# Head halves alternating in the matmuls of a recurrence: preparation and scan output of an RWKV-7 mixer, with a zero-padded operand

## The chip, the cores and the metric

The kernel runs on one core of one Trainium2 chip. The metric is the device time of one execution in microseconds (us). The kernel before takes 4488.92 us, the median of 3 runs from 4473.94 to 4512.09.

## What is computed

Two layers of a backbone with four head groups side by side (neighbourhood attention, latent attention, RWKV-7 time mixing in both directions, differential attention), each followed by a gated MLP, over 1024 latent and 256 context tokens of width 1024 in float32. The change lies in the RWKV-7 group, whose reference is a scan over tokens, per head a 64 x 64 state S:

```python
def rwkv7_scan(r, decay, k, v, a, b, s0, reverse):
    def step(S, inp):
        r_t, w_t, k_t, v_t, a_t, b_t = inp
        sa = jnp.einsum('bhij,bhj->bhi', S, a_t)
        S = S * w_t[:, :, None, :] + sa[..., None] * b_t[:, :, None, :] + v_t[..., None] * k_t[:, :, None, :]
        return S, jnp.einsum('bhij,bhj->bhi', S, r_t)
    ...
```

with decay, a and k made per token from a small low-rank projection (`w0[d] + jnp.tanh(wd) @ w_up[d]`, `a0[d] + ad @ a_up[d]`). It runs forwards and backwards (d = 0, 1), over the context first, then over the latent tokens; layer 1 needs no output for the context.

## The kernel before, in words

The scan is done in chunks of 64 tokens. Four heads are held as two pairs p; a pair's two heads are the halves e = 0, 1 of the 128 partitions (partitions 64e to 64e + 63). A slot is 128 tokens, two chunks; ten slots per layer. The index u = 2p + c names pair and chunk.

`mix` builds one layer's work from generators that are pulled in turn at given rates: a main one (projections, then attention) and sides. A scheduler then sets the order in which each engine issues its instructions, by its own estimate of their times and by what they wait for; every engine works its queue in order. The sides that the change touches:

- `prep_gen`, preparation, beside the projections (lines L140 to L142, tiles psd and psv). Per slot, `load` (L312) fetches the slot's columns into z and the inputs of the low-rank projection into zm, 33 partitions (32 and a row of ones, memset in L319); `partA` (L322) makes, for j = 0 (decay) and j = 1 (a), four matmuls into a PSUM tile pu each (L330), both with partitions 0 to 32 as operands. `partB` then makes BK and ARM; `gram(d)` (L432) multiplies them per half e, four matmuls of 64 partitions into a tile pg each (L437), first all of e = 0, then all of e = 1; `gout` masks the results into NT, RB and ARM; `tb(d)` (L451) transposes BK per half into pbt (L456). PSUM tiles of preparation come from two pools of two buffers. A slot ends with stores to DRAM (rnt, rsg).
- `lanes_gen` inverts small triangular blocks with VectorE (L543, L544) and merges them with 32 x 32 matmuls (L576, L578).
- `rw_step_gen`, the scan, 20 steps per layer, beside the attention (L788 logits psL, L958 exp, L996 transposes psT, L1017 products psV) and the modulation matmuls of later stages (L1541, adaps). A step: eight matmuls into pd (L653), ScalarE copies them to Dt (L656), eight into psa (L665), ScalarE and VectorE copy the halves into V1 (L667, L668), eight into pss (L674), VectorE makes the next state from pss and tmp (L682). V1 holds, for each e, psa's half on the partitions of e and a copy of VS's other half on the others (L649, on GpSimd, which also makes tmp, L659). Then comes the step's output py: for each direction d, pair p and half e one matmul over all 128 partitions (L692: VS by ARM, output on the 64 partitions of e) and one over the 64 partitions of e alone that adds to it (L693: V1 by RB). ScalarE copies py out (L697). In the step's PSUM tile pall, pss takes the place of pd, and py that of psa.

A matmul of float32 operands appears in the trace as two records of TensorE (two passes), a transpose as one.

```python
for e in range(2):
    r = slice(64 * e, 64 * e + 64)
    MM(py[r, d, p], VS[:, c, e, d, p], ARM[:, d, e, u, 64:P], start=True, stop=False)
    MM(py[r, d, p], V1[r, e, d, p], RB[r, d, u], start=False, stop=True)
```

Of the kernel before, what the change touches and what calls it, by code (L numbers as in the profile page):

```python
# [17 lines left out]
P = 128  # L18
# [22 lines left out]
class K:  # L41
# [241 lines left out]
    def prep_gen(self, l, rw, pool, psA, psB, F):  # L283
# [6 lines left out]
        uwa = pool.tile([33, 2, 512], F32, tag="rwuwa", name="rwuwa")  # L290
        nc.sync.dma_start(uwa, A["rwuwa"][l])
# [20 lines left out]
        def load(sl):  # L312
            s = self.SLOT[sl]
            z = pool.tile([P, 3, 2, P], F32, tag="sz", name="sz", bufs=2)
            zm = pool.tile([33, 2, P], F32, tag="szm", name="szm", bufs=2)
            nc.sync.dma_start(z, self.rzd[:, :, :, s * P:(s + 1) * P])
            for j in range(2):
                nc.sync.dma_start(zm[0:32, j], self.rzm[32 * j:32 * j + 32, s * P:(s + 1) * P])
            nc.gpsimd.memset(zm[32:33], 1.0)  # L319
            st[sl] = dict(z=z, zm=zm)  # L320

        def partA(sl):  # L322
# [4 lines left out]
            for j in range(2):  # L327
                pu = pst([P, 4, P], "pu")
                for dp in range(4):
                    MM(pu[:, dp], uwa[:, j, dp * P:(dp + 1) * P], zm[:, j], start=True, stop=True)  # L330
                ps.append(pu)
# [61 lines left out]
        def partB(sl):  # L393
# [38 lines left out]
            def gram(d):  # L432
                for e in range(2):
                    r = slice(64 * e, 64 * e + 64)
                    g[e] = psb([P, 4, P], "pg")
                    for u in range(4):
                        MM(g[e][:, u], BKf[r, d, u, 64 * e:64 * e + P], ARf[r, d, e, u], start=True, stop=True)  # L437
# [13 lines left out]
            def tb(d):  # L451
                for e in range(2):
                    r = slice(64 * e, 64 * e + 64)
                    g[2 + e] = psb([P, 4, 64], "pbt")
                    for u in range(4):
# [143 lines left out]
    def rw_step_gen(self, l, pool, sgp, yp, psp, ptag, need_ctx, F):  # L599
# [7 lines left out]

        def seg(i):
# [26 lines left out]
        for step in range(20):  # L635
# [32 lines left out]
            nc.vector.tensor_copy(V1[64:128, 1], psa[64:128])  # L668
            yield
# [14 lines left out]
            if i < 2 and not need_ctx:  # L684
                yield
                continue
            for d in range(2):
                for p in range(2):
                    u = 2 * p + c
                    for e in range(2):  # L690
                        r = slice(64 * e, 64 * e + 64)
                        MM(py[r, d, p], VS[:, c, e, d, p], ARM[:, d, e, u, 64:P], start=True, stop=False)  # L692
                        MM(py[r, d, p], V1[r, e, d, p], RB[r, d, u], start=False, stop=True)  # L693
# [1592 lines left out]
```

## Time and profile before

| | us |
|---|---|
| time, median of 3 runs (lowest, highest) | 4488.92 (4473.94, 4512.09) |
| profiled execution, span from first to last instruction | 4497.2 |
| TensorE busy | 4274.2 (95%) |
| VectorE busy | 2883.1 (64%) |
| ScalarE busy | 1984.4 (44%) |
| GpSimd busy | 754.3 (17%) |
| mean granted TensorE clock | 0.942 of full speed |

The profile is that of one execution on the chip. The profiled execution's own time is given by its span alone, which lies within the range of the timed runs. Matmuls overlap each other, and their ends are modelled, so a busy share of TensorE isn't a share of its peak; the distance between the starts of two matmuls is measured. Preparation runs from about 100 to 560 us (layer 0) and 2440 to 2860 us (layer 1), the scan from 600 to 1000 and from 3000 to 3325 us.

### The profile page before, as it was taken

How to read it: one execution, taken by the hardware profiler on the slowest of the kernel's cores; microseconds unless marked ns; L12 is line 12 of the kernel's file. 1: busy time of each engine (PE TensorE's matmuls, PEld its weight loads, DVE VectorE, ACT ScalarE, POOL GpSimd, SP SyncE). 2: the span in 40 equal slices, each digit the busy share in tenths (PEclk: the TensorE clock that was granted, in tenths of full speed). 3: DMA queues.
4: the chain of work that ended last, by engine and by line, in shares of the span. 5: the costliest groups of instructions: out<-in, count | busy, mean ns of one | idle time of the engine just before them, and what ended most of it. 6: DMA issues, size and time to landing. Idle time of an engine off the chain costs nothing.

```text
span 4497.2 us, 76564 instructions
## 1 busy us (share of the span) xinstructions
PE 4274.2 (95%) x29152; PEld 3473.1 (77%) x29152; DVE 2883.1 (64%) x5946; ACT 1984.4 (44%) x4386; POOL 754.3 (17%) x1224
## 2 busy tenths in 40 slices
PE   6999979999999999899998999979999999999998
PEld 4887857677677778788887887857786777788998
DVE  6678675546576766655556668675556676657666
ACT  4444434334465544433334444434434555434443
POOL 3244121112211011100001334121112101111000
PEclk7999978889999999999998999978899999999999
DMA  6344685553433243221213334685434432333322
GB/s 207 131 136 163 188 230 170 175 157 109 131 98 114 77 129 115 84 64 61 66 62 118 130 129 162 191 252 171 159 89 129 135 95 80 116 104 130 95 93 77
DMA packets 422598, 575.77 MB, mean 128 GB/s; under 512 B 109078, under 2 KB 287638, under 8 KB 420696
## 3 DMA queue, kind: packets, MB, share of 16 engines
q1 hardware_dynamic: 422232, 570.88, 41.1%
q8 instruction: 230, 3.77, 0.3%
q14 instruction: 136, 1.11, 0.1%
HBM read 430.84 MB, written 139.92 MB: 127 GB/s over the span
## 4 chain that ended last, share of the span: by engine, by line
PE 78%; DVE 11%; DMA 5%; issue 2%; ACT 2%; SPq 1%; POOL 1%; POOLq 0%; DVEq 0%; ACTq 0%
PE psm L140 12%; PE psm L141 12%; PE psm L142 11%; PE psV L1017 6%; PE psT L996 5%; PE psd L140 2%; PE psd L141 2%; PE psd L142 2%; PE psL L788 2%; DVE lpr L543 2%; PE pall L693 2%; PE pall L692 2%; PE pso L140 1%; PE pso L142 1%; PE pso L141 1%
## 5 line engine op out<-in xcount | busy, mean ns | idle before, releaser
L141 PE MATMUL psm<-h_l,whi 128*128 128x512 f32 (+1 forms) x2112 | 711.1, 337 | 9.1 <-DVE h_l L258 9.0
L140 PE MATMUL psm<-h_h,whi 128*128 128x512 f32 (+1 forms) x2112 | 713.7, 338 | 4.0 <-ACT h_h L257 4.0
L142 PE MATMUL psm<-h_h,wlo 128*128 128x512 f32 (+1 forms) x2112 | 709.2, 336 | 0.0
L1873 DVE SCALAR_TENSOR_TENSOR x<-psm,mod,x 128x258 f32<-128x258 f32 (+2 forms) x616 | 326.8, 555 | 285.2 <-PE psm L142 284.8
L958 ACT ACTIVATE sm_P<-psL,sm_n 128x512 f32<-128x512 f32 (+1 forms) x672 | 392.5, 593 | 251.7 <-DVE sm_n L949 225.2
L947 DVE TENSOR_REDUCE sm_m<-psL 128x1 f32<-128x512 f32 (+1 forms) x640 | 354.5, 579 | 180.8 <-PE psL L788 90.0
L141 PEld LDWEIGHTS psm<-h_l,whi 128*128 128x128 f32 x2112 | 399.4, 189 | 54.3 <-DVE h_l L258 12.1
L140 PEld LDWEIGHTS psm<-h_h,whi 128*128 128x128 f32 x2112 | 399.5, 189 | 53.9 <-ACT h_h L257 5.7
L142 PEld LDWEIGHTS psm<-h_h,wlo 128*128 128x128 f32 x2112 | 399.2, 189 | 43.8 <-issue 0.3
L140 PE MATMUL psm<-gh,dhi 128*128 128x510 f32 (+3 forms) x1056 | 364.3, 347 | 8.6 <-ACT mb L1837 4.0
L133 ACT ACTIVATE whi<-wst 128x1024 fp32r<-128x1024 f32 x176 | 186.5, 1060 | 403.3 <-PE psm L141 380.0
L141 PE MATMUL psm<-gl,dhi 128*128 128x510 f32 (+3 forms) x1056 | 357.2, 339 | 0.0
L142 PE MATMUL psm<-gh,dlo 128*128 128x510 f32 (+3 forms) x1056 | 356.9, 338 | 0.0
L134 DVE TENSOR_TENSOR wlo<-wst,whi 128x1024 fp32r<-128x1024 f32 x176 | 214.7, 1220 | 174.7 <-ACT whi L133 174.6
L996 PE MATMUL psT<-ident,sm_P 128*128 128x128 f32 x1744 | 303.9, 297 | 9.2 <-DVE sm_P L986 5.3
L1017 PE MATMUL psV<-PT,V 128*64 128x128 f32 x3488 | 308.0, 290 | 1.3 <-DVE sm_n L949 0.6
L1017 PEld LDWEIGHTS psV<-PT,V 128*64 128x64 f32 x3488 | 215.7, 141 | 85.6 <-issue 67.6
L996 PEld LDWEIGHTS psT<-ident,sm_P 128*128 128x128 f32 x1744 | 212.1, 150 | 76.2 <-issue 28.5
L140 PEld LDWEIGHTS psm<-gh,dhi 128*128 128x128 f32 x1056 | 199.4, 189 | 42.5 <-ACT a L1829 8.7
L1006 ACT ACTIVATE PT<-psT 128x512 f32<-128x512 f32 (+2 forms) x300 | 152.8, 526 | 153.7 <-PE psT L996 151.1
L142 PEld LDWEIGHTS psm<-gh,dlo 128*128 128x128 f32 x1056 | 200.1, 189 | 21.7
L141 PEld LDWEIGHTS psm<-gl,dhi 128*128 128x128 f32 x1056 | 200.2, 190 | 17.6 <-issue 0.5
(381 smaller groups left out, 9575.6 us busy)
## 6 DMA issues: line engine op xcount, KB each, us to landing
wst<-in_w_up_dram SPq DMA_DIRECT2D x176, 512.0 KB
wst<-in_w_down_dram SPq DMA_DIRECT2D x88, 512.0 KB
adw<-in_ada_w_dram SPq DMA_DIRECT2D x80, 512.0 KB
SG<-rsg SPq DMA_DIRECT2D x40, 896.0 KB
wst<-in_w_out_dram SPq DMA_DIRECT2D x96, 256.0 KB
rsg<-ARM SPq DMA_DIRECT2D x20, 1024.0 KB
K<-dfk SPq DMA_DIRECT2D x16, 960.0 KB
wst<-in_w_rw_dram SPq DMA_DIRECT2D x28, 512.0 KB
```

What stands on the lines that cost most here:

```text
L133: nc.scalar.activation(hi[:, :n], st[:, :n], AF.Copy)
L134: nc.vector.tensor_tensor(out=lo[:, :n], in0=st[:, :n], in1=hi[:, :n].bitcast(F32), op=ALU.subtract)
L140: mm(out, ah, bh, start=first, stop=False)
L141: mm(out, ah, bl, start=False, stop=False)
L142: mm(out, al, bh, start=False, stop=last)
L543: TT(out=pr[:n, 0:t, 0:t], in0=XT[:n, 0:t, 0:t], in1=M[:n, None, 0:t, t].to_broadcast([n, t, t]), op=ALU.mult)
L947: nc.vector.tensor_reduce(out=m[:, j, i:i + 1], in_=src, axis=AX.X, op=ALU.max)
L958: ACT(Pt[:, off:off + n], s["L"][j][t][:, to:to + n], AF.Exp, bias=neg, accum_out=sm[:, j, i:i + 1])
L996: nc.tensor.transpose(pt[:, j], Ph[:, (bb + j) * P:(bb + j + 1) * P], self.ident)
L1006: ACT(dst, src, AF.Copy)
L1017: nc.tensor.matmul(s["po"][64 * h:64 * h + 64, 0], V[:, kts[i], h], s["PT"][h][:, i], start=i == 0, stop=i == nk - 1, tile_position=(0, 64 ...
L1873: STT(out=x[:, s:e], in0=ps[:, s:e], scalar=mod[:, v, 40 + m:41 + m], in1=x[:, s:e], op0=ALU.mult, op1=ALU.add)
```

## The change

The two inputs of the low-rank projection lie on different partition halves now (zm and uwa: j = 0 on partitions 0 to 32, j = 1 on 64 to 96), and in pu, gram and tb the inner loop runs over the halves, so that consecutive matmuls in the source go to different row halves of the array. In the scan output, both matmuls with VS come first and then both that add to them, and the second operand V1 is replaced by SZ, a tile with V1's half on the partitions of e and zeros on the others, zeroed once per layer and filled by two GpSimd copies per step. The second matmul so reads all 128 partitions, as the first does.

```diff
-        uwa = pool.tile([33, 2, 512], F32, tag="rwuwa", name="rwuwa")
-        nc.sync.dma_start(uwa, A["rwuwa"][l])
+        uwa = pool.tile([P, 512], F32, tag="rwuwa", name="rwuwa")
+        for j in range(2):
+            nc.sync.dma_start(uwa[64 * j:64 * j + 33], A["rwuwa"][l][:, j])
...
-            zm = pool.tile([33, 2, P], F32, tag="szm", name="szm", bufs=2)
+            zm = pool.tile([P, P], F32, tag="szm", name="szm", bufs=2)
             nc.sync.dma_start(z, self.rzd[:, :, :, s * P:(s + 1) * P])
             for j in range(2):
-                nc.sync.dma_start(zm[0:32, j], self.rzm[32 * j:32 * j + 32, s * P:(s + 1) * P])
-            nc.gpsimd.memset(zm[32:33], 1.0)
+                nc.sync.dma_start(zm[64 * j:64 * j + 32], self.rzm[32 * j:32 * j + 32, s * P:(s + 1) * P])
+                nc.gpsimd.memset(zm[64 * j + 32:64 * j + 33], 1.0)
...
             for j in range(2):
-                pu = pst([P, 4, P], "pu")
-                for dp in range(4):
-                    MM(pu[:, dp], uwa[:, j, dp * P:(dp + 1) * P], zm[:, j], start=True, stop=True)
-                ps.append(pu)
+                ps.append(pst([P, 4, P], "pu"))
+            for dp in range(4):
+                for j in range(2):
+                    r = slice(64 * j, 64 * j + 33)
+                    MM(ps[j][:, dp], uwa[r, dp * P:(dp + 1) * P], zm[r], start=True, stop=True)
...
             def gram(d):
                 for e in range(2):
-                    r = slice(64 * e, 64 * e + 64)
                     g[e] = psb([P, 4, P], "pg")
-                    for u in range(4):
+                for u in range(4):
+                    for e in range(2):
+                        r = slice(64 * e, 64 * e + 64)
                         MM(g[e][:, u], BKf[r, d, u, 64 * e:64 * e + P], ARf[r, d, e, u], start=True, stop=True)
...
             def tb(d):
                 for e in range(2):
-                    r = slice(64 * e, 64 * e + 64)
                     g[2 + e] = psb([P, 4, 64], "pbt")
-                    for u in range(4):
+                for u in range(4):
+                    for e in range(2):
+                        r = slice(64 * e, 64 * e + 64)
                         nc.tensor.transpose(g[2 + e][:, u], BKf[r, d, u, 64 * e:64 * e + P], self.ident[r, r])
...
+        def step_y(i):
+            return i >= 2 or need_ctx
+
+        SZ = pool.tile([P, 2, 2, 2, 64], F32, name="SZ", bufs=1)
+        for e in range(2):
+            nc.gpsimd.memset(SZ[64 - 64 * e:128 - 64 * e, e], 0.0)
+
...
             nc.vector.tensor_copy(V1[64:128, 1], psa[64:128])
+            if step_y(i):
+                for e in range(2):
+                    nc.gpsimd.tensor_copy(SZ[64 * e:64 * e + 64, e], V1[64 * e:64 * e + 64, e])
...
-            if i < 2 and not need_ctx:
+            if not step_y(i):
...
                     u = 2 * p + c
+                    r = [slice(64 * e, 64 * e + 64) for e in range(2)]
                     for e in range(2):
-                        r = slice(64 * e, 64 * e + 64)
-                        MM(py[r, d, p], VS[:, c, e, d, p], ARM[:, d, e, u, 64:P], start=True, stop=False)
-                        MM(py[r, d, p], V1[r, e, d, p], RB[r, d, u], start=False, stop=True)
+                        MM(py[r[e], d, p], VS[:, c, e, d, p], ARM[:, d, e, u, 64:P], start=True, stop=False)
+                    for e in range(2):
+                        MM(py[r[e], d, p], SZ[:, e, d, p], RB[:, d, u], start=False, stop=True)
```

In the changed kernel the lines lie lower: pu is L333, gram L440, tb L460, the scan's pd L664, psa L676, the SZ copies L682, pss L688, the output L706 and L708.

The order of TensorE at the first scan output of layer 0, before. SG is the tile in which ARM, RB and BT are loaded, V_5908 the V1 of that step:

```order
L674 MATMUL pall<-V_5908,SG 64x64 x8
L788 MATMUL psL<-K,Q 128x512
L788 MATMUL psL<-K,Q 128x256
L692 MATMUL pall<-SG,VS 64x64
L693 MATMUL pall<-SG,V_5908 64x64
L692 MATMUL pall<-SG,VS 64x64
L693 MATMUL pall<-SG,V_5908 64x64
```

The same place in the changed kernel:

```order
L1011 MATMUL psT<-ident,sm_P 128x128 x4
L1556 MATMUL adaps<-adw,sc_60 32x256 x4
L1032 MATMUL psV<-PT,V 64x128 x8
L706 MATMUL pall<-SG,VS 64x64 x2
L708 MATMUL pall<-SG,SZ 64x64 x2
L706 MATMUL pall<-SG,VS 64x64 x2
L708 MATMUL pall<-SG,SZ 64x64 x2
```

The sixteen matmuls went one by one between the two lines; now two of L706 (e = 0, 1) and two of L708 follow each other.

The order of TensorE at the first gram of layer 0, before (pg_1140 is the tile of e = 0, pg_1145 of e = 1):

```order
L142 MATMUL psd_1313<-H0_h0_101,wlo_1123 128x512
L330 MATMUL pu_1172<-szm_1076,rwuwa_904 128x128 x4
L437 MATMUL pg_1140<-ARM_1082,BK_1081 128x128 x4
L437 MATMUL pg_1145<-ARM_1082,BK_1081 128x128 x4
L344 MATMUL pk_1218<-sel2_420,ksq_1196 128x2 x2
```

And now (pg_1143 is the tile of e = 0, pg_1144 of e = 1):

```order
L333 MATMUL pu_1171<-szm_1078,rwuwa_904 128x128 x4
L440 MATMUL pg_1143<-ARM_1085,BK_1084 128x128 x2
L440 MATMUL pg_1144<-ARM_1085,BK_1084 128x128 x2
L440 MATMUL pg_1143<-ARM_1085,BK_1084 128x128
L440 MATMUL pg_1144<-ARM_1085,BK_1084 128x128
L440 MATMUL pg_1143<-ARM_1085,BK_1084 128x128
L440 MATMUL pg_1144<-ARM_1085,BK_1084 128x128
L346 MATMUL pk_1221<-sel2_420,ksq_1199 128x2 x2
```

The halves alternate five times here, not seven times as in the source. At other places the scheduler puts the four of e = 0 ahead of the four of e = 1, as before.

The order of GpSimd in the scan of layer 0, before (o_ss is the sum of squares of the differential attention's output, V1 the L649 copies, stmp the products of L659):

```order
L649 COPY V1_6696<-VS_6338 64x256 x2
L1039 TENSOR_TENSOR o_ss_7016<-o_ss_7016,mhalf_68 128x2
L1040 TENSOR_TENSOR o_ss_7016<-o_ss_7016,rec_6374 128x2
L659 TENSOR_TENSOR stmp_6698<-VS_6338,W_6339 64x256 x2
L649 COPY V1_7116<-VS_6338 64x256 x2
L1037 TENSOR_TENSOR o_ss_7325<-o_ss_7325,rec_6658 128x2
```

And now:

```order
L670 TENSOR_TENSOR stmp_6545<-VS_6085,W_6086 64x256 x2
L1054 TENSOR_TENSOR o_ss_7355<-o_ss_7355,mhalf_68 128x2
L632 COPY W_7232<-Wc_94 128x2x2 x2
L1055 TENSOR_TENSOR o_ss_7355<-o_ss_7355,rec_6684 128x2
L682 COPY SZ_5885<-V1_6543 64x256 x2
L660 COPY V1_7144<-VS_6360 64x256 x2
L670 TENSOR_TENSOR stmp_6724<-VS_6360,W_6361 64x256 x2
L682 COPY SZ_5885<-V1_6722 64x256 x2
```

The two SZ copies of a step come in between the products of that step and the V1 copies for a later one, behind what o_ss work stands there.

## Rows read from the trace of the kernel before

**Rows 1.** The page's part 1: engine, busy us, share of the span, instructions.

```profile
PE 4274.2 (95%) x29152; PEld 3473.1 (77%) x29152; DVE 2883.1 (64%) x5946; ACT 1984.4 (44%) x4386; POOL 754.3 (17%) x1224
```

**Rows 2.** Busy time by stretch: length, engines, granted clock, DMA share, GB/s.

```profile
100.00:560.00 460.00, 442.50 (x2930) 370.10 (x2929) 326.56 (x588) 210.57 (x442) 147.33 (x212) 0.96 0.49 156
600.00:1000.00 400.00, 378.08 (x3598) 271.99 (x3599) 223.51 (x531) 155.58 (x463) 66.33 (x131) 0.82 0.61 181
1000.00:1400.00 400.00, 392.47 (x2514) 285.28 (x2512) 266.01 (x720) 206.07 (x541) 69.80 (x85) 0.97 0.38 112
3000.00:3325.00 325.00, 317.17 (x3183) 233.60 (x3183) 179.66 (x450) 140.46 (x415) 54.81 (x118) 0.88 0.54 162
```

**Rows 3.** Chain that ended last, shares by line: 600 to 1000, 3000 to 3325.

```profile
by line: PE psT L996 12.7%; PE psV L1017 12.2%; PE pall L693 11.8%; PE pall L692 11.7%; PE adaps L1541 7.5%; PE psL L788 5.7%; PE psL L140 4.6%; PE pall L653 3.5%; PE psL L141 3.4%; PE psL L142 3.4%; DVE sm_m L947 3.2%; DMA Q<-dfq 3.1%; PE 
...
by line: PE psT L996 14.8%; PE psV L1017 14.7%; PE pall L693 10.7%; PE pall L692 10.4%; PE psL L788 6.7%; PE adaps L1541 5.9%; PE psL L140 5.5%; PE psL L142 4.3%; PE psL L141 4.3%; PE pall L653 3.7%; PE pall L665 3.5%; PE pall L674 2.6%; DV
```

**Rows 4.** L674's durations (ns min/median/max); TensorE's timeline, its first row at half clock.

```profile
L674 PE MATMUL pall<-V,SG x640: 219/222/369, 618.5 to 3320.0; 128*64 128x64 f32 x160
...
618.51 1.12 PE L674 MATMUL pall<-V,SG 128*64 128x64 f32 x16 [1.35 <-DVE V L668]
...
945.76 1.31 PE L1017 MATMUL psV<-PT,V 128*64 128x128 f32 x18
...
953.55 0.69 PE L674 MATMUL pall<-V,SG 128*64 128x64 f32 x16
...
955.49 0.33 PE L692 MATMUL pall<-SG,VS 128*64 128x64 f32 x2
955.75 0.32 PE L693 MATMUL pall<-SG,V 64*64 64x64 f32 x2
...
960.04 1.97 PE L996 MATMUL psT<-ident,sm_P 128*128 128x128 f32 x8
```

**Rows 5.** Busy time in the 36 blocks of L692 and L693: first, last, sum.

```profile
622.57:629.02 6.45, 6.45 (x33) 4.58 (x32) 6.38 (x8) 0.00 (x0) 3.51 (x4) 0.50 1.09 242
...
3320.03:3324.09 4.06, 4.06 (x37) 2.98 (x33) 0.00 (x0) 0.00 (x0) 0.00 (x0) 1.00 0.00 0
sum 163.75, PE 163.27 PEld 118.90 DVE 61.32 ACT 30.65 POOL 34.06; mean PE 4.54 PEld 3.30 DVE 1.70 ACT 0.85 POOL 0.95
```

**Rows 6.** Timeline of VectorE and ScalarE: V1's second half, an exp.

```profile
950.73 0.43 DVE L668 COPY V<-pall 64x256 f32<-64x256 f32 x1 [0.98 <-ACT V L667]
...
956.39 0.68 ACT L958 ACTIVATE sm_P<-psL,sm_n 128x512 f32<-128x512 f32 x1
```

**Rows 7.** Busy time in the 22 stretches at half clock: first, last, sum.

```profile
672.10:682.40 10.30, 10.30 (x61) 7.91 (x59) 3.85 (x6) 3.28 (x12) 2.90 (x4) 0.50 0.72 178
...
3324.30:3327.70 3.40, 3.40 (x14) 2.95 (x12) 1.85 (x3) 0.28 (x1) 0.00 (x0) 0.50 0.35 104
sum 170.90, PE 168.50 PEld 121.50 DVE 62.35 ACT 53.20 POOL 22.64; mean PE 7.66 PEld 5.52 DVE 2.83 ACT 2.42 POOL 1.03
```

**Rows 8.** Timeline of TensorE in preparation, at full clock, with the next start.

```profile
115.03 2.02 PE L330 MATMUL pu<-szm,rwuwa 33*128 33x128 f32 x16
...
169.79 1.71 PE L437 MATMUL pg<-ARM,BK 64*128 64x128 f32 x16
171.43 0.50 PE L142 MATMUL psd<-H_h,wlo 128*128 128x512 f32 x1
...
233.96 1.16 PE L437 MATMUL pg<-ARM,BK 64*128 64x128 f32 x8
235.04 0.38 PE L140 MATMUL psv<-whi,H_h 128*128 128x256 f32 x1
```

**Rows 9.** Groups by line: out<-in, shapes, count, busy us, mean ns, idle before.

```profile
L437 PE MATMUL pg<-ARM,BK 64*128 64x128 f32 x640 | 85.8, 294 | 11.4 <-POOL ARM L405 11.4
L649 POOL COPY V<-VS 64x256 f32<-64x256 f32 x80 | 37.1, 467 | 181.6 <-PE pall L693 67.8 <-issue 54.4 <-DMA VS<-rvt 39.7
```

**Rows 10.** Waits of GpSimd: total us, times, longest.

```profile
POOL o_ss L1037 <- DVE o_ss L1035: 189.3, 30, 27.8
```

## The prediction

> **What bounds the kernel now.** I read the page's engine line first: TensorE is busy for 95% of the span, every other engine far less [rows 1]. That number is a modelled one, so the next view is the busy time by stretch [rows 2]. While the scan runs (600 to 1000 us in layer 0, 3000 to 3325 us in layer 1) TensorE is busy 378 of 400 and 317 of 325 us, VectorE at most 56%, ScalarE at most 43%, GpSimd 17%. The stretch behind it, 1000 to 1400, has the same attention without the scan, and TensorE is as full there, but its granted clock is 0.97 against 0.82 and 0.88 with the scan. Third, the chain that ended last in the two scan stretches [rows 3]: the scan output's two lines, L692 and L693, hold 23.5% of the 400 us (94 us) and 21.1% of the 325 (69 us). So these matmuls stand on the path nearly whole. Fourth, the timeline of one block tells why [rows 4]: each row is two records (one float32 matmul is two passes), L692 uses a 128x64 tile of the array and L693 a 64x64 tile, and the next row begins 0.26 us later; a whole block takes 4.06 us for its 32 records [rows 5], 127 ns each. L674, sixteen records of 128x64 whose output halves alternate, needs 0.69 us in all: without the last one's own 0.22 us (its median duration) that is 31 ns from start to start. Same operand sizes, a quarter of the time; the tile shape that changes at each pair is the difference.
>
> **The change part by part.**
>
> *Scan output.* Before, 16 matmuls per step go 128x64, 64x64, 128x64 and so on: 16 changes of shape. After, L708 reads all 128 partitions of SZ, whose other half is zero, so all 16 have one shape, and e alternates in pairs, which is the form of L674. There are 36 blocks (20 steps in layer 0, 16 in layer 1, where the two context segments need no output). The windows over them sum to 163.75 us, 4.55 each; one at full clock takes 4.06 [rows 5]. A new block at full clock: 32 records by 31 ns, about 1.0 us, and 0.2 for one change of shape at its entry (the 0.26 us of a pair less 2 x 31 ns): 1.2. With the present mix of clocks (4.55 / 4.06 = 1.12) 36 blocks take 48 us. Removed: 163.75 - 48 = 116 us of TensorE.
>
> How much of that stays a gain? After the block that starts at 955.49 come eight transposes of sm_P at 960.04 [rows 4]; an exp for such a tile begins at 956.39 and takes 0.68 [rows 6]. If the block ends at 956.7, they may stand 0.4 us for that exp and about as long for the next: some 0.7 of 3.35 us saved is lost again. So I keep four fifths: 93 us. The bounds are all of it (116, as VectorE and ScalarE are half idle) and half of it (58).
>
> *The clock.* Between 652 and 1000 us and between 3010 and 3330 us the granted clock fell to half (1.2 of 2.4 GHz) 22 times, in stretches of 170.9 us together [rows 7], and each of the 22 begins inside one of these blocks or at most 1.1 us behind it. The blocks' own excess over full clock is 163.75 - 36 x 4.06 = 17.6 us. L674's sixteen take 1.12 us instead of 0.69 at half clock [rows 4], so half clock costs 38% of the time spent in it; the 17.6 us thus are 46 us at half, of which 13 belong to two blocks in the slow beginning of the stage (the first takes 6.45 [rows 5]). So 170.9 - 33 = 138 us of other work ran at half clock, and 52 us come back if the falls end with the blocks. Other small matmuls stay in these stages (L653, L665, L674, the 32-column adaps), and a TensorE that now and then waits may lose its clock as well. I take two thirds: 35 us; bounds 0 and 52.
>
> *Gram, projection and transposes in preparation.* The source alternates e, but the scheduler decides the order of issue, and counted in the order of the changed program it keeps this only in part. Of the 40 gram calls (eight matmuls, 16 records), 22 had their halves apart before and 18 joined with one alternation; after, 10 are apart, 6 have one, 14 three, 8 five and 2 seven. For pu, matmuls followed by one of the other tile go from 14 to 98 of 160. For the transposes pbt from 0 to 5 of 320: that edit all but disappears. Prices: a gram half alone takes 1.08 us, two apart 2.16; joined with one alternation 1.64 [rows 8]. A full alternation doesn't occur before; its bounds are 1.0 (two streams wholly beside each other) and 1.64. I take 1.3 for three, 1.15 for five, 1.0 for seven: before 22 x 2.16 + 18 x 1.64 = 77, after 10 x 2.16 + 6 x 1.64 + 14 x 1.3 + 8 x 1.15 + 2 x 1.0 = 61, which saves 16 us of the 85.8 us that L437 is busy [rows 9]. pu is 16 records in 2.02 us and all on one half of the rows [rows 8]; halved where it alternates, 20 calls save about 12 us. In preparation TensorE is busy 442 of 460 us [rows 2], but VectorE 71% and each slot ends in a store and a load, so I count half: 14 of 28 us; bounds 0 and 28.
>
> *What is added.* Two copies V1 to SZ per step on GpSimd, 0.467 us each by the like copy L649 [rows 9]: 72 copies, 34 us on an engine that has 334 us free in the first scan stretch. They hang on V1, whose second half is done at 951.16 in the step shown, 4.33 us ahead of its block [rows 6, 4]; two copies need 0.93. Behind them on GpSimd stand the V1 half copies and the tmp products of the next steps, which now wait mostly for VS. A second memset of one partition per slot and one more weight DMA per layer lie beside other work: nothing.
>
> Sum: 93 + 35 + 14 = 142 us off a profiled span of 4497.2. That span is 8 us over the median of the timed runs (4488.92, from 4473.94 to 4512.09), so I subtract from the median: **4347 us**.
>
> A rule that speaks against the first term: the new block's matmuls use all 128 rows and differ in columns only, and the records of L674, which do just that, start every 31 ns [rows 4]. The Trainium skill, "TensorE: Matmul & The Clock Gate", section "Part 3: Packing small matmuls — row/col tiling", says that a weight load overlaps a running matmul only when the row group differs. By that rule such a pair would go no faster than L1017's records, 61 ns each in the row at 945.76 [rows 4]. The sum by the row is 4347, by the rule 4376 (below); the trace disagrees with it.
>
> **The rivals.**
> - *All of it.* The attention fills every freed slot and the clock stays up: 116 + 52 + 28 = 196 us, 4293 us. For it: the clock of 0.97 in the same attention without scan. Against it: in-order queues always leave some waits. 0.20.
> - *The waits take over.* TensorE stands for the softmax and for V1 and VS where it worked before, and its clock falls in those gaps instead: half of the block's gain, nothing of the clock, a quarter of preparation: 58 + 7 = 65 us, 4424 us. For it: VectorE 56%. Against it: 1000 to 1400 shows TensorE at 392 of 400 us with VectorE at 67% [rows 2]. 0.16.
> - *Columns alone don't overlap.* 61 ns a record makes 2.2 us per block, 1.0 more, 36 us, four fifths of it 29: 4376 us. 0.05.
> - *Nothing moves.* The scan's own chain sets the stage and TensorE's blocks fill its gaps: 4489 us. Against it: the blocks are 21 to 23% of the chain [rows 3], and attention that is not done here has to be done later. 0.05.
> - *Slower: the copies arrive late.* They queue on GpSimd behind the o_ss rows, which waited 30 times for VectorE, 6.3 us on average, 27.8 at most [rows 10]. A late SZ stops L708, and with it all of TensorE's queue. The slack is 4.33 - 0.93 = 3.4 us; to lose the 142 us and 1% more (45 us) every block must stand 5.2 us, so the copies must be 8.6 us late in each step. At 10 us late: 36 x 6.6 = 238, less 142: 4585 us. Against it: V1 and tmp pass the same queue today, and the block isn't kept from starting. 0.04.
>
> **How the numbers follow.** The forecast has 0.50, the rivals in their order 0.20, 0.16, 0.05, 0.05 and 0.04. The range reaches from below the first (4270, as a reordered program also moves by some 15 us) to just over the second (4430). A measurement of this kernel can tell about 1% from no change; faster by more than that: 0.50 + 0.20 + 0.16 + 0.05 = 0.91, within 1%: 0.05, slower: 0.04.
>
> **What would show it.** Right: L706 and L708 with 31 ns between records at full clock, blocks of about 1.2 us, their share of the chain from 22% to some 6%; a granted clock of 0.93 or more in the scan's stretches, and both of these shorter by some 60 us; gram calls of 1.0 to 1.3 us where they alternate; pbt as before. Wrong: L708 waiting for SZ, records 50 to 60 ns apart at full clock, a clock that still falls behind the blocks, or more idle time on TensorE ahead of psT and psL than the blocks gave back.

## The result, and the profile after

The changed kernel takes 4359.5 us (median of 4 runs, 4352.19 to 4369.82) against 4492.11 us before, timed beside it: 0.9701 of the time before, 95% interval [0.9675, 0.9727]. The forecast was 4347 us, with a range of 4270 to 4430. The profiled execution has a span of 4358.3 us where the one before had 4497.2, so 138.9 us went.

The page's part 1, as [rows 1], and the busy time by stretch, as [rows 2]:

```profile
PE 4084.0 (94%) x29152; PEld 3334.3 (77%) x29152; DVE 2871.4 (66%) x5946; ACT 1984.1 (46%) x4386; POOL 803.7 (18%) x1320
```

```profile
100.00:560.00 460.00, 439.35 (x2935) 366.82 (x2935) 318.09 (x583) 210.52 (x440) 147.67 (x221) 0.94 0.48 157
600.00:1000.00 400.00, 359.36 (x4198) 263.82 (x4199) 279.08 (x675) 188.57 (x560) 96.22 (x187) 0.91 0.65 197
1000.00:1400.00 400.00, 392.60 (x2294) 288.82 (x2289) 264.87 (x677) 211.34 (x529) 65.73 (x87) 0.97 0.40 118
3000.00:3325.00 325.00, 313.13 (x3394) 234.00 (x3392) 214.31 (x601) 161.26 (x478) 73.30 (x133) 0.98 0.51 149
```

As many matmul records as before (x29152) cost TensorE 190 us less. The share of busy time hardly moved, 95% to 94%, though the kernel is 3% faster: the column after the engines, the clock, says more. In the two scan stretches it rose from 0.82 and 0.88 to 0.91 and 0.98, and 600 more records of matmuls begin in the first 400 us (4198 for 3598). In preparation (100 to 560) it fell from 0.96 to 0.94.

The groups by line of the new output, of the copies that feed it, and of gram, as [rows 9]; then TensorE's timeline at one output, as [rows 4]:

```profile
L706 PE MATMUL pall<-SG,VS 128*64 128x64 f32 x576 | 39.0, 231 | 0.0
L708 PE MATMUL pall<-SG,SZ 128*64 128x64 f32 x576 | 37.7, 227 | 0.0
L682 POOL COPY SZ<-V 64x256 f32<-64x256 f32 x72 | 30.6, 426 | 268.3 <-ACT V L678 246.7 <-DVE V L679 17.9 <-PE psT L1011 2.2
L440 PE MATMUL pg<-ARM,BK 64*128 64x128 f32 x640 | 75.3, 301 | 15.1 <-POOL ARM L407 14.9
```

```profile
915.38 0.28 PE L706 MATMUL pall<-SG,VS 128*64 128x64 f32 x4
915.49 0.29 PE L708 MATMUL pall<-SG,SZ 128*64 128x64 f32 x4
915.61 0.29 PE L706 MATMUL pall<-SG,VS 128*64 128x64 f32 x4
...
916.19 0.29 PE L708 MATMUL pall<-SG,SZ 128*64 128x64 f32 x4
916.41 0.44 PE L1011 MATMUL psT<-ident,sm_P 128*128 128x128 f32 x2
```

Eight rows of four records, 0.117 us apart: 29 ns a record on average, and 1.03 us from the first to the next work, where it was 4.06 [rows 5]. Record by record the starts come in pairs, one of each half e, 7 ns apart, and a pair every 58 ns. The last column of L706 and L708 in the groups is 0.0: neither waited for anything. Below are the sum over the 36 blocks, as the last row of [rows 5], and, as [rows 7], the stretches at half clock in the same two windows of time, 652 to 1000 and 3010 to 3330 us (two of them and the sum; the changed kernel's scan ends at 928 and at 3197):

```profile
sum 42.63, PE 39.69 PEld 37.30 DVE 30.35 ACT 10.81 POOL 19.58; mean PE 1.10 PEld 1.04 DVE 0.84 ACT 0.30 POOL 0.54
```

```profile
679.69:686.52 6.83, 4.03 (x41) 2.74 (x43) 1.29 (x5) 0.60 (x1) 0.00 (x0) 0.50 0.84 258
...
857.18:860.60 3.42, 3.42 (x35) 2.62 (x35) 2.61 (x5) 1.07 (x4) 3.12 (x5) 0.50 1.08 265
...
sum 37.55, PE 34.32 PEld 26.46 DVE 18.21 ACT 15.10 POOL 5.62; mean PE 4.90 PEld 3.78 DVE 2.60 ACT 2.16 POOL 0.80
```

Seven stretches with 37.55 us stand where 22 with 170.9 us were. Counted from the first pd to the last output instead, in both layers, half clock went from 248 to 70 us. TensorE's timeline shows what stands at these two: the first begins while TensorE waits 5.53 us for Q, the second right behind a wait of 1.17 us; the output blocks at 685.05 and 858.76 merely lie inside.

```profile
682.49 0.76 PE L803 MATMUL psL<-K,Q 96*128 96x512 f32 x1 [5.53 <-DMA Q<-dfq]
...
857.18 0.79 PE L140 MATMUL psL<-K,Q 96*128 96x512 f32 x1 [1.17 <-ACT sm_P L973]
```

The chain that ended last, 3000 to 3325 us, as [rows 3]. L692 and L693 held 21.1% of it; L706 and L708 are not among the lines that fit the row. Its pieces give them 3.3% together, and 4.4% from 2909 to 3197, while the scan runs. (The changed kernel's chain can be followed back to 2580 us only, so the first stretch has no such row.)

```profile
by line: PE psV L1032 20.7%; PE psT L1011 18.2%; PE psL L140 5.5%; PE psL L873 4.6%; PE psL L142 4.2%; PE psL L141 4.2%; PE psL L872 3.8%; PE psL L803 3.6%; DMA oy<-ryd 2.8%; PE adaps L1556 2.6%; DMA adw<-in_ada_w_dram 2.3%; PE psV L1038 2.
```

Where the 138.9 us lie, by the starts of pu, pbt, pd and the last output in the traces (us; layer 0, layer 1, and the sum of both differences):

| | before | changed | difference |
|---|---|---|---|
| preparation: first pu to last pbt | 365.2, 357.1 | 367.4, 365.4 | +10.5 |
| last pbt to the scan's first pd | 127.3, 132.7 | 144.6, 143.6 | +28.2 |
| scan: first pd to last output | 386.8, 356.9 | 298.3, 288.3 | -157.1 |
| all other stretches | 2771.2 | 2750.7 | -20.5 |

So the scan gave more than the whole result; preparation became no shorter, and the scan begins later behind it. The last row is to be read with care: the stretch from the last output of layer 1 to the end, in which no version differs, takes 1158 to 1204 us in the profiles of this case, so a difference of some 20 us in a single profile can come from there. The experiments take this apart.

### The profile page after: what moved, and what is told of

Its sections match the earlier page's. It is cut to its first block, busy times and chain, and to the rows that moved or that the text cites. A ratio compares the mean times of both kernels' runs of the same rounds, so it can differ in the third digit from the quotient of the medians.

```text
span 4358.3 us, 76687 instructions
## 1 busy us (share of the span) xinstructions
PE 4084.0 (94%) x29152; PEld 3334.3 (77%) x29152; DVE 2871.4 (66%) x5946; ACT 1984.1 (46%) x4386; POOL 803.7 (18%) x1320
## 5 line engine op out<-in xcount | busy, mean ns | idle before, releaser
L142 PE MATMUL psm<-gh,dlo 128*128 128x510 f32 (+3 forms) x1056 | 357.1, 338 | 0.0
L1011 PE MATMUL psT<-ident,sm_P 128*128 128x128 f32 x1744 | 291.8, 289 | 6.8 <-DVE sm_P L1001 3.3
L1011 PEld LDWEIGHTS psT<-ident,sm_P 128*128 128x128 f32 x1744 | 203.2, 145 | 72.4 <-issue 33.2
```

Source lines behind the costliest of these rows:

```text
L142: mm(out, al, bh, start=False, stop=last)
L1011: nc.tensor.transpose(pt[:, j], Ph[:, (bb + j) * P:(bb + j + 1) * P], self.ident)
```

## The experiments

Line numbers differ a little from version to version. **Each half of the change alone.** scan_only is the kernel before with the scan output's part of the diff (SZ, its zeroing, its copies, the new order); prep_only is the changed kernel with that part taken back:

```diff
...
-                    r = [slice(64 * e, 64 * e + 64) for e in range(2)]
                     for e in range(2):
-                        MM(py[r[e], d, p], VS[:, c, e, d, p], ARM[:, d, e, u, 64:P], start=True, stop=False)
-                    for e in range(2):
-                        MM(py[r[e], d, p], SZ[:, e, d, p], RB[:, d, u], start=False, stop=True)
+                        r = slice(64 * e, 64 * e + 64)
+                        MM(py[r, d, p], VS[:, c, e, d, p], ARM[:, d, e, u, 64:P], start=True, stop=False)
+                        MM(py[r, d, p], V1[r, e, d, p], RB[r, d, u], start=False, stop=True)
```

> The scan output as in the changed kernel (order of the pairs and SZ), preparation as before. Theory A (the change of tile shape inside the scan output is the whole of the gain, by the block's own time and by the clock that fell with it): about 140 us under the kernel before, so 4350 us or a little less, both scan stretches shorter by 65 to 90 us, and preparation as long as before. Rival B (the alternation in preparation gives a part of the gain): at most 125 us under before, and slower than the changed kernel by 10 to 20 us.

> Preparation as in the changed kernel, scan output as before. Theory A with the prediction's own term: 10 to 15 us under before. What the changed kernel's trace suggests (both preparation stretches got 2 to 8 us longer, and the scan began later behind them): no gain, or up to 15 us slower. Rival B: 15 us or more faster.

Measured: the scan output alone 4336.88 us, 0.9658 [0.963, 0.9686]; preparation alone 4514.86 us, 1.004 [1.0013, 1.0067], so 0.4% slower than before. The scan output alone is faster than the whole change. Run again on one chip, with five rounds:

> The changed kernel unaltered, on the same chip as the next two, so that they can be set against it: 4355 to 4365 us, the first pd of layer 0 at about 630 us.

> The scan output's change alone, unaltered, on the same chip. If the preparation's part costs some 20 us: 4335 to 4342 us, and its interval lies clear of the whole change's. If what lay between the two was a difference between chips: within 8 us of the changed kernel.

The changed kernel has 4364.3 us, 0.9714 [0.9695, 0.9732], and the scan output alone 4341.47 us, 0.9672 [0.9649, 0.9696]: 22.8 us apart by the medians, with intervals that only just touch. In the first profile of the scan output alone the scan takes 297.5 and 276.6 us, 169.6 less than before; each of the other stretches, taken by itself, is within 4 us of before.

**What in the block gave the time.** Four versions with the preparation of before. In the first, y_pairs, V1 stays on 64 partitions and only the order changes: two of one shape, two of the other, 8 runs of a shape in a block instead of 16. Against the kernel before:

```diff
+                    r = [slice(64 * e, 64 * e + 64) for e in range(2)]
                     for e in range(2):
-                        r = slice(64 * e, 64 * e + 64)
-                        MM(py[r, d, p], VS[:, c, e, d, p], ARM[:, d, e, u, 64:P], start=True, stop=False)
-                        MM(py[r, d, p], V1[r, e, d, p], RB[r, d, u], start=False, stop=True)
+                        MM(py[r[e], d, p], VS[:, c, e, d, p], ARM[:, d, e, u, 64:P], start=True, stop=False)
+                    for e in range(2):
+                        MM(py[r[e], d, p], V1[r[e], e, d, p], RB[r[e], d, u], start=False, stop=True)
```

> Kernel before, but in the scan output the two halves of the first matmul come first and then the two halves of the second, without SZ: the second operand stays V1 on 64 partitions. Theory A: changes of shape fall from 16 to 8 per block, a block at full clock from 4.06 to about 2.5 us (32 records by 31 ns and 8 changes by 0.2 us), the clock falls less often; 60 to 80 us under before, half of the gain. Rival C (it is the alternation of the halves that counts, not the shape): blocks of 1.0 to 1.2 us and the whole gain, 130 us or more.

The second, y_pad, pads (SZ is made and filled as in the changed kernel), but keeps the order of before, so that both matmuls of a half follow each other:

```diff
-                        MM(py[r, d, p], V1[r, e, d, p], RB[r, d, u], start=False, stop=True)
+                        MM(py[r, d, p], SZ[:, e, d, p], RB[:, d, u], start=False, stop=True)
```

> Kernel before, but with SZ as second operand and the order as before (each half's two matmuls behind each other). Theory A: no change of shape inside a block; four records on the same columns in a row cost up to 60 ns each, so a block takes 1.2 to 1.9 us; 100 to 130 us under before. Rival C (the alternation counts): little of the gain, under 40 us.

The third, y_halves, pads too, but puts all eight matmuls of e = 0 ahead of those of e = 1 (the first edit, against scan_only). The fourth, scan_twice, is scan_only with its block issued twice (the second).

```diff
-            for d in range(2):
-                for p in range(2):
+            for e in range(2):
+                for d in range(2):
+                    for p in range(2):
...
```

```diff
                         MM(py[r[e], d, p], SZ[:, e, d, p], RB[:, d, u], start=False, stop=True)
+                    for e in range(2):
+                        MM(py[r[e], d, p], VS[:, c, e, d, p], ARM[:, d, e, u, 64:P], start=True, stop=False)
+                    for e in range(2):
+                        MM(py[r[e], d, p], SZ[:, e, d, p], RB[:, d, u], start=False, stop=True)
```

> The scan output's change alone with zero-padded operand and one tile shape, but all eight matmuls of e = 0 come first and then all eight of e = 1, so that the output's column halves don't alternate. If two column halves run side by side (in the trace of the padded versions each half's own records start 58 ns apart, those of the two halves together 29): 32 records at 58 ns make about 1.9 us a block instead of 1.08, 36 x 0.8 = 29 us more TensorE time, and some 4360 to 4366 us. If one tile shape alone sets the 29 ns and the alternation does nothing: 1.1 us a block and 4337 us.

> The scan output's change alone, and its 16 matmuls are issued twice in a row (the second pass starts afresh and writes the same result), preparation as before. This measures what 1 us of TensorE in this place is worth. If TensorE's time there stands on the path whole: 36 blocks of 64 records instead of 32 add 36 x 1.0 = 36 us, so some 4373 us against 4337 of the version with one pass. If much of what the smaller blocks gave back only fills waits (the forecast kept four fifths, its rival half): 18 to 29 us more, 4355 to 4366. If other engines set the scan's pace now: under 10 us more. If the clock falls because of a change of tile shape inside the block, a dense block of twice the length keeps the clock and time at half clock in the two scan stretches stays under 100 us; if it falls because of many small matmuls, it goes well over that.

The windows over the blocks of y_pairs, y_halves and scan_twice, their sums in this order, and under them a piece of TensorE's timeline of y_pairs and of y_halves:

```profile
sum 81.93, PE 81.42 PEld 59.94 DVE 51.46 ACT 22.23 POOL 33.95; mean PE 2.20 PEld 1.62 DVE 1.39 ACT 0.60 POOL 0.92
```

```profile
sum 73.18, PE 72.12 PEld 69.34 DVE 51.44 ACT 17.92 POOL 37.31; mean PE 1.95 PEld 1.87 DVE 1.39 ACT 0.48 POOL 1.01
```

```profile
sum 80.13, PE 76.72 PEld 74.14 DVE 45.33 ACT 27.26 POOL 36.42; mean PE 2.07 PEld 2.00 DVE 1.23 ACT 0.74 POOL 0.98
```

```profile
932.23 0.34 PE L692 MATMUL pall<-SG,VS 128*64 128x64 f32 x4
932.49 0.33 PE L694 MATMUL pall<-SG,V 64*64 64x64 f32 x4
932.75 0.34 PE L692 MATMUL pall<-SG,VS 128*64 128x64 f32 x4
```

```profile
921.65 0.28 PE L701 MATMUL pall<-SG,VS 128*64 128x64 f32 x2
921.77 0.28 PE L702 MATMUL pall<-SG,SZ 128*64 128x64 f32 x2
921.88 0.28 PE L701 MATMUL pall<-SG,VS 128*64 128x64 f32 x2
```

| | runs of a shape, halves | one block at full clock (median), us | time, us | ratio to before |
|---|---|---|---|---|
| before | 16, in pairs | 4.11 | | 1 |
| y_pairs | 8, alternating | 2.11 | 4387.44 | 0.9766 [0.9732, 0.98] |
| y_halves | 1, apart | 1.83 | 4378.54 | 0.9748 [0.9714, 0.9782] |
| scan_twice | 1, alternating, twice | 2.02 | 4379.84 | 0.9756 [0.9726, 0.9787] |
| y_pad | 1, in pairs | 1.13 | 4340.78 | 0.967 [0.9636, 0.9703] |
| scan output alone | 1, alternating | 1.08 | 4336.88 | 0.9658 [0.963, 0.9686] |

Three readings. First, both edits of the block count, in this order: padding alone (y_pad) gives what the whole edit gives, and alternation alone (y_pairs) gives some two thirds. y_pad needs no new order since its halves change every two matmuls anyway; it is only with eight of one half in a row that a record takes 58 ns (0.117 us for two in y_halves) instead of 29. Second, in y_pairs four records with a change of shape at their end take 0.26 us, in the padded block 0.117: a change costs 0.14 us at full clock there. With the 0.117 us that two records of one half take, that also makes the 0.26 us from row to row in the kernel before [rows 4]. Third, scan_twice measures what TensorE's time is worth here: 80.13 - 43.7 = 36.4 us more in the blocks (43.7 is the sum over the blocks of the scan output alone) made 43 us more by the first runs and 38 by the second, with intervals that leave some 17 us either way. The scan stretches in the profiles say it more closely: against those of the scan output alone they are 35 to 38 us longer in scan_twice, 23 to 26 in y_halves for 29.5 us more in the blocks, 32 to 35 in y_pairs for 38.2. So 0.8 to 1.0 of TensorE's time at this place is on the path.

The expectations missed here in size: y_pairs and y_pad came out 113 and 159 us under before, more than expected; y_halves and scan_twice took 13 and 7 us more than the most that was expected.

**What preparation cost.** Two versions have the new scan output and one part of the new preparation each. scan_gt is scan_only with the alternation in gram and tb (pu, zm and uwa as before); scan_pu has pu, zm and uwa as in the changed kernel, gram and tb as before. The edit of gram, which scan_gt has and scan_pu hasn't:

```diff
                 for e in range(2):
-                    r = slice(64 * e, 64 * e + 64)
                     g[e] = psb([P, 4, P], "pg")
-                    for u in range(4):
+                for u in range(4):
+                    for e in range(2):
+                        r = slice(64 * e, 64 * e + 64)
```

> The scan output's change and the alternation in gram and tb, the projection pu as before. In the order of this program the scan's first loads of VS and XB stand where they stand in the version with the scan output alone, ahead of most of the attention's loads. If the late start of the scan in the changed kernel (VS behind Q, K, V and the mask on SyncE's queue) is what cost the 20 us there: about 4337 us, the first pd at 605 to 617 us. If the alternating gram itself costs (both its tiles wait for ARM of e = 1, and TensorE's clock falls in these waits): 4348 to 4360 us, and preparation some 5 us longer in each layer. If the forecast's term holds (8 us for gram): 4329 us.

> The scan output's change and the projection pu on two row halves (with its loads and memsets), gram and tb as before. The scan's first load of VS stands early on SyncE's queue here. If the queue's order is what cost in the changed kernel: 4325 to 4340 us, first pd no later than 617 us. If the projection's edit costs by itself (two more memsets and one more load, two PSUM tiles claimed at once): 4348 to 4360 us. If the forecast's term holds (half of 12 us): 4331 us, with pu at 60 ns between records where it alternates, against 126 before.

Measured 4347.87 us, 0.9675 [0.9638, 0.9712], and 4340.49 us, 0.9667 [0.9633, 0.97]: neither part by itself differs from the scan output alone by more than the intervals leave (some 16 us either way), for better or worse. In both the scan's first pd comes at 606 to 607 us, where it was before (607.57). Only with both parts it is late, and that holds without the new output, too: preparation alone has it at 627.78. SyncE's and TensorE's timelines of the changed kernel's second profile show what is late (SPq is SyncE's queue):

```profile
596.04 5.06 SPq L630 DMA_DIRECT2D SG<-rsg  x4
...
602.54 6.60 SPq L799 DMA_DIRECT2D Q<-dfq  x1
609.18 3.47 SPq L816 DMA_DIRECT2D K<-mlk  x2
...
613.30 6.59 SPq L847 DMA_DIRECT2D msk<-in_na_mask_dram  x1
...
621.23 4.43 SPq L629 DMA_DIRECT2D VS<-rvt  x2
```

```profile
632.22 0.92 PE L664 MATMUL pall<-VS,SG 128*64 128x64 f32 x8 [3.13 <-issue]
```

And of the scan output alone, second profile:

```profile
590.46 0.91 SPq L792 DMA_DIRECT2D K<-dfk  x2
...
592.07 1.35 SPq L625 DMA_DIRECT2D VS<-rvt  x2
```

```profile
604.92 0.78 PE L660 MATMUL pall<-VS,SG 128*64 128x64 f32 x8 [0.88 <-DMA SG<-rsg]
```

In the first the scheduler put the scan's VS loads behind loads of the attention, so that they are issued 29 us later. TensorE's own order moved with them: of the attention's records, 18 of psL, 10 of psT and 2 of psV stand between the last pbt and the first pd in both profiles of the changed kernel, and 4 of psL alone in those of the scan output alone; the first pd itself then waits 3.13 us. Two more versions test the late start. after_actq takes the changed kernel and issues the first loads of VS (shown) and of XB on ScalarE's queue; scan_late takes scan_only and gives its first loads a later place in the scheduler's order.

```diff
-                    nc.sync.dma_start(VS[q, :, e, d].rearrange("s c p i -> s c (p i)"), vt[e])
+                    (nc.sync if i else nc.scalar).dma_start(VS[q, :, e, d].rearrange("s c p i -> s c (p i)"), vt[e])
```

```diff
+        q = self.tc.cur_priority
+        self.tc.cur_priority = max(q +1500, 0)
         seg(0)
+        self.tc.cur_priority += q - max(q +1500, 0)
```

> The changed kernel; only the scan's very first loads of VS and XB are issued on ScalarE's queue instead of SyncE's, where they stand behind the attention's loads. Up to the scan's first matmul TensorE's order is the same. If the late loads are what the preparation's part costs: the first pd at 605 to 615 us instead of 630, likewise in layer 1, and 4335 to 4345 us. If the cost lies in preparation itself (gram's waits, the pool of PSUM tiles): the scan starts earlier but the end stays at 4352 to 4362 us, since what the attention does at the stage's beginning is only done later. If the loads wait for something else: pd at 630 us as before, 4360 us.

> The scan output's change alone, preparation untouched; only the place of the scan's very first loads (VS, SG, XB of its first segment) in the scheduler's order is put back, so that on SyncE's queue they stand behind loads of the attention (Q, V and K) as in the changed kernel, though not behind its mask. If the late start of the scan is the price of the preparation's part: the first pd at 615 to 632 us instead of 605 and a like shift in layer 1, and 4348 to 4362 us. If the cost lies inside preparation: 4335 to 4345 us whatever the first pd does.

after_actq went the other way: 4409.19 us, 0.9805 [0.9786, 0.9825]. ScalarE's timeline has the reason, and the row of L629 on its queue (an instruction that waits for a semaphore: count, ns min/median/max, first and last start):

```profile
609.96 5.26 ACTq L629 DMA_DIRECT2D VS<-rvt  x2
...
625.32 0.69 ACT L973 ACTIVATE sm_P<-psL,sm_n 128x512 f32<-128x512 f32 x1 [40.13 <-DMA VS<-rvt]
```

```profile
L629 ACTq EVENT_SEMAPHORE  x2: 38/10458/20879, 589.0 to 2921.7; - x2
```

The load is issued at 609.96 only, and behind it ScalarE's first exp stood for 40.13 us; the scan began at 645.80. ScalarE's queue had come to the load at 589.0 and waited there for 20.9 us; one of the two semaphores that it waited for got its last count at 609.89, from the attention's load V<-vtm that SyncE's queue had issued at 594.90. So on the other queue, too, the load stayed behind a load of the attention. The experiment failed as an undo, but it lengthened what it was to shorten. scan_late, with nothing of the preparation's edit in it, hit in the first pd (630.50) and in the direction, and overshot in the time: 4371.52 us, 0.9731 [0.9694, 0.9768], where 4348 to 4362 was expected. SyncE's row of these loads, and TensorE's first of the scan:

```profile
612.47 11.00 SPq L625 DMA_DIRECT2D VS<-rvt  x6
```

```profile
630.50 0.54 PE L663 MATMUL pall<-VS,SG 128*64 128x64 f32 x8 [1.49 <-issue]
```

Four profiled executions with the same scan output, and how long the stretch from the last pbt to the first pd is in both layers together:

| | that stretch, us | span, us |
|---|---|---|
| scan output alone, again | 249.8 | 4335.0 |
| scan_late | 288.7 | 4369.8 |
| changed kernel, again | 289.5 | 4370.1 |
| after_actq | 326.4 | 4398.0 |

Against the first row each us by which the scan starts later costs 0.8 to 0.9 us at the end. Against the other profile of the scan output alone (259.1 and 4331.6 us) it is 1.0 to 1.3, so the price of a us is known to be near one and no better. The times say the same without a price: the versions with an early start take 4337 to 4348 us, those with a late one 4360 to 4409. What is lost in between is seen in the busy time from 600 to 640 us, the scan output alone first, then the changed kernel, then scan_late:

```profile
600.00:640.00 40.00, 27.54 (x222) 19.58 (x223) 37.20 (x61) 13.96 (x42) 16.26 (x20) 0.50 1.07 310
```

```profile
600.00:640.00 40.00, 17.96 (x71) 10.05 (x71) 38.02 (x64) 13.56 (x41) 5.39 (x8) 0.50 0.98 291
```

```profile
600.00:640.00 40.00, 15.37 (x56) 8.61 (x57) 37.05 (x61) 11.53 (x35) 3.21 (x4) 0.54 1.06 301
```

The DMA engines are full there (0.98 to 1.07) and TensorE has little else to do: 222 records of matmuls begin in the one case, 71 and 56 in the others. scan_late also moves other instructions behind this place, and TensorE's order with them (13 records of psL, 10 of psT and 2 of psV ahead of the first pd of layer 0). So a start that late, with what moves along with it, cost some 30 us without preparation's edit; whether the loads' place or TensorE's order makes the start late was not separated.

## Why the prediction was right in its sum, and the steps that failed

*The new block.* Forecast 1.2 us at full clock and 116 us of TensorE removed; measured 1.08 and 163.75 - 42.63 = 121. The reading of L674 in [rows 4] as the new block's price held. The rule that spoke against it didn't: the Trainium skill, "TensorE: Matmul & The Clock Gate", section "Part 3: Packing small matmuls — row/col tiling", has weight loads overlap only where the row group differs. Here all records use all rows, and those of alternating column halves start 29 ns apart on average, those of one half 58 ns. So two column halves do run side by side; what part of the 58 ns is weight load the starts don't show. The forecast named the change of shape as the whole difference to L674. It is the larger part: with one shape but no alternation (y_halves) a block still takes 1.83 us.

*How much of it stays.* "I keep four fifths: 93 us" was somewhat too little. The waits for the exp that I had counted behind each block, 0.7 us each and 25 in all, did not grow: TensorE's waits ahead of psT in the two scans went from 5.4 to 4.1 us. Waits of another kind did, ahead of adaps for its weights (0.5 to 21.3 us), and TensorE stands idle 51 us in the two scans where it stood 35. So in the changed kernel 16 of the 121 us were lost again, by another wait than the one counted.

*The clock.* Forecast 35 us (bounds 0 and 52). Half clock in the two windows went from 170.9 to 37.55 us, of which 3.3 us lie in the blocks. So the other work at half clock went from 138 to 34 us, and 38% of the difference is 40 us, more than forecast and inside its bounds. Counted over the whole scans the other work at half clock went from 202 to 66.5 us, which makes 52 us. That gives 121 + 52 - 16 = 157 us, what was measured, against 128 forecast for block and clock. The fit is better than such a sum deserves: for the scan output alone it gives 148 to 152 where 166 and 170 were measured, and since the changed kernel's scan starts later, some of the half clock at its beginning (to 642.14 us) now lies ahead of the scan. The clock of 0.93 asked for came in the second stretch (0.98), not in the first (0.91), whose first 42 us are part of that half clock.

*Preparation.* This is the step that failed: "I count half: 14 of 28 us". TensorE's busy time for pu, gram and pbt did fall, from 171.2 to 150.6 us by their groups (gram 85.8 to 75.3 [rows 9 and above]; pu and pbt below, before and changed; pbt was to stay as before). A gram with its halves alternating took 1.42 us where it wasn't interrupted (309.92 to 311.34), against 1.64 for [rows 8]' joined one and 1.0 to 1.3 forecast.

```profile
L330 PE MATMUL pu<-szm,rwuwa 33*128 33x128 f32 x320 | 43.1, 281 | 1.4 <-DMA szm<-rzm 1.3
L456 PE MATMUL pbt<-ident,BK 64*128 64x64 f32 x320 | 42.3, 241 | 11.7 <-DVE ARM L445 8.3 <-DVE krs L356 3.4
...
L333 PE MATMUL pu<-szm,rwuwa 33*128 33x128 f32 x320 | 37.7, 306 | 3.1 <-DMA szm<-rzm 2.1 <-issue 1.0
L460 PE MATMUL pbt<-ident,BK 64*128 64x64 f32 x320 | 37.6, 240 | 11.7 <-ACT zt L1332 4.5 <-DVE ARM L448 3.8 <-DVE krs L358 3.3
```

But preparation (first pu to last pbt) became no shorter: in the four profiles with both parts it takes 364 to 368 us in layer 0 and 360 to 365 in layer 1, in the eight with the old one 362 to 371 and 352 to 358. The traces show what took the place of the 20 us. Between the first pu and the last pbt now stand 867 and 857 records of the projection psd (layer 0 and 1) in all four profiles with both parts, 846 and 826 in the eight with the old preparation: 52 records more, about 12 us at the 0.23 us between their starts (an estimate). And TensorE stands idle 37 to 41 us there, 22 to 29 with the old preparation. So none of the saved TensorE time came off preparation's length. And behind it the scan came late. The forecast's price list had a saving for the matmuls and none for what the scheduler does with a reordered program: 28 us later starts and 10 us in preparation, of which some 20 came back elsewhere (in part perhaps by the spread of the last stretch). A second price was not counted either: with both halves' tiles open, a gram whose second half isn't ready stands in its middle, as the timeline of the changed kernel shows.

```profile
309.92 1.49 PE L440 MATMUL pg<-ARM,BK 64*128 64x128 f32 x16
311.34 0.71 PE L378 MATMUL pkb<-ident,kbc 128*128 128x128 f32 x4
...
455.79 0.71 PE L440 MATMUL pg<-ARM,BK 64*128 64x128 f32 x4 [0.27 <-POOL ARM L407]
460.59 2.07 PE L440 MATMUL pg<-ARM,BK 64*128 64x128 f32 x12 [4.10 <-POOL ARM L407]
```

Four records, 4.1 us for ARM, and twelve records at half clock. L440 waits 15 us in all, 4 more than L437 did [rows 9], so this is a small part. How the scheduler comes to start the scan late only with both parts stays open.

*What is added.* Nothing, as forecast: 72 copies at 0.426 us (0.467 assumed), and no wait of L708 for SZ. In the step shown they are done 3.0 us ahead of the block:

```profile
911.51 0.86 POOL L682 COPY SZ<-V 64x256 f32<-64x256 f32 x2 [7.59 <-ACT V L678]
```

That takes the ground from the slower rival. "Columns alone don't overlap" fell with the block's own rows, "the waits take over" and "nothing moves" with the scan's 157 us. "All of it" was close about the scan: its 116 + 52 = 168 us are near what the scan output alone gave (4497.2 - 4331.6 = 165.6 in the first profile, 162.2 in the second, 153 to 163 by the medians). The forecast of 4347 us came near 4359.5 by luck in its parts: a scan term 29 us too small and a preparation term some 32 us too favourable (14 gained; 157.1 - 138.9 = 18 lost) cancelled. The forecast's 142 us stand against 138.9 in the profile; the rest of the 12 us lies between profiles and medians.

The best version of all is the scan output alone: 4337 and 4341 us in two sets of runs, some 20 us under the changed kernel; y_pad and scan_pu, at 4341 and 4340 us, can't be told from it.

## What to carry to other kernels

Small float32 matmuls that alternate between two tile shapes cost four times here what the same matmuls cost in one shape: look in the timeline for rows of one or two records that are 0.26 us apart, and try padding the smaller operand with zeros. Once the shape is one, see that column halves change at least every second matmul. And in a program that a scheduler orders, price a reordering by what it does to the order of the next stage, not only by the matmuls it joins: here the scan began 23 to 27 us later in layer 0, nothing of the saving on joined matmuls was left, and only taking the edits one at a time showed it.

## What the runs showed that was not expected

- Matmuls on alternate column halves run side by side, also with all 128 rows in use: 29 ns a record on average against 58.
- The clock's falls don't go with the number of changes of shape alone. From the first pd to the last output, both layers, half clock lasts 248 us before and 197 in the version with the preparation's part alone (both 16 runs of a shape a block, 4.1 us long), 109 in y_pairs (8 runs, 2.1 us), 112 in y_halves, 98 in scan_twice (one run, 1.8 and 2.0 us), 119 in y_pad (one run, 1.1 us) and 85 and 103 in the two profiles of the scan output alone. Versions with the same block differ by as much as these (scan_pu has 137), so from 8 runs down no difference stands out. What in the long block lets the clock fall stays open.
- Loads put on ScalarE's queue stopped ScalarE until they could be issued: its first exp stood for 40 us, and the kernel took 45 us more than the changed kernel on the same chip.
